# Fifteen instead of twelve weight pairs by seven products in the down projection, with GpSimd taking part of VectorE's work

## The chip, the cores and the metric

The kernel runs on one core of one Trainium2 chip. A core has TensorE (PE in the profile, with PEld for its weight loads), VectorE (DVE), ScalarE (ACT), GpSimd (POOL) and SyncE (SP), which here only issues DMAs. The metric is the device time of the core in microseconds, median of three runs; lower is better.

## The reference

One layer of an encoder block over 256 tokens of width 2048, in float32: RMS norm, one input projection, a bidirectional state-space mixer beside a pooling mixer, an output projection, a gated conv-MLP, and a gate by a per-layer embedding. The part that the change is about is the MLP and the gate after it:

```
hn = rmsnorm(h, ffn_norm_pre)
up = hn @ w_up                      # 256 x 2048 by 2048 x 11264
gate, val = split(up, 2)
hidden = gelu(dwconv3(gate)) * val  # 256 x 5632
h = h + rmsnorm(hidden @ w_down, ffn_norm_post)        # 5632 x 2048
gate = sigmoid(rmsnorm(h, ple_norm_pre) @ w_ple_gate)  # 2048 x 2048
out = h + rmsnorm(gate * (p @ w_ple), ple_norm_post)
```

## The kernel before, in words

**Products.** All large products keep float32 accuracy with a faster matmul type. Each operand is cut in a high part (the value rounded to float32r, a cast on ScalarE) and a low part (the value minus its high part, a subtraction on VectorE), and a product is the sum of three matmuls: high by high, high by low, low by high. `split` (lines 141 to 154) does this for a weight block; its two tags `whi` and `wlo` have five buffers each. Raw weights arrive in the tag `raw`, three buffers, by DMAs that SyncE issues in program order.

**Stages.** The input projection (dtu, xbc, z), the output projection (wo), the up projection (22 blocks of gate and 22 of value features, names ga and va, by `feature_pairs`), the down projection (dn), the small product ple, and the gate (gt). Down, gate and wo go by `token_major`: the 2048 output columns are done in two halves of 1024; in each half the loop goes over pairs of 128-row weight blocks. Down has 44 blocks, so 22 pairs per half, numbered u = 0 to 21. A half holds its sums in eight PSUM banks.

**Two ways for a pair.** A regular pair takes 2 blocks x 2 token halves x 2 column halves x 3 matmuls = 24 matmuls of 128x128 by 128x512, and two weight splits of 128x1024. A fast pair (listed in `dn_fast`, `gt_fast`) takes the 2x2 block product by seven products instead of eight (`seven_products`, from line 239), so 21 matmuls; it needs four weight splits (one of 128x512, three of 128x1024), of which two are of sums of weight blocks, and four sums of activation blocks with their own high and low parts (`pair_sums`, line 774: four small VectorE operations, a ScalarE cast, a VectorE subtraction). After the last fast pair of a half, `combine` (line 269) puts the products together once.

**Sums of weights.** `block_sums` (line 208) makes them ahead of time: during the up stage each of its jobs loads a 1 MB pair into a page, adds with three VectorE operations (`add_blocks`, lines 235 to 237), and stores the page to DRAM; down loads it back. The list `work` holds jobs by slot; `aside` runs one slot after each half of a `feature_pairs` call, 88 slots in up. There are 28 such pairs (24 of down, 4 of the gate), one every three slots; the last two stay in their pages.

**Activations of down.** `get_hid` (line 899) makes the high and low part of the 128x512 piece of the hidden activations that a pair needs, into the tag `hs` with two buffers: a cast on ScalarE (line 903) and a subtraction on VectorE (line 904). `hid_sums` makes the activation sums of a fast pair; in half 0 those of four pairs (`dn_keep`) are kept in pages and used again in half 1. Pages (tag `pg`, 13 buffers of 128x2048) hold the hidden activations (six), what is kept, and the loaded sums.

**Order.** A scheduler of the framework orders each engine's instructions in advance from estimated durations and priorities; each engine then runs its list strictly in order, with semaphores between engines.

**GpSimd before.** It does one multiplication per up slab (line 885), a few operations of the mixer (lines 673 and 685), the small norm factors, and in half 1 of down one DMA that adds in flight (`first_gate`, line 949). In down it is otherwise idle.

Of the kernel before, what the change touches and what calls it, by code (L numbers as in the profile page):

```python
# [16 lines left out]
P = 128  # L17
L = 256
# [33 lines left out]
def build(nc, a, out):  # L52
    x = a["x"][0]
    w_in, w_out, w_up = a["w_in"][0], a["w_out"][0], a["w_ffn_up"][0]
    w_down, w_gate, w_ple = a["w_ffn_down"][0], a["w_ple_gate"][0], a["w_ple"][0]
    out = out[0]

    with tile.TileContext(nc) as tc, \
# [37 lines left out]
        c_dt = DSSD + 1536  # L96
        r0 = wp.tile([P, 2048], F32, tag="raw", bufs=3, name="dtur0")
        for n in range(2):
            first = ins(nc.scalar.dma_start(r0[:, n * 352:(n + 1) * 352],
                                            w_in[:P, c_dt + n * 352:c_dt + (n + 1) * 352]))  # L100
# [55 lines left out]
        def raw(name, src, a_, b_):  # L156
            r = wp.tile([P, 2048], F32, tag="raw", bufs=3, name=name)
            if src is None:
                return r
            last["dma"] = load(r[:, :a_ * b_].rearrange("p (a b) -> p a b", a=a_), src, True)  # L160
            return r
# [46 lines left out]
        def block_sums(name, w, c0, k, held):  # L208


            pg = []

            def fetch():
                r = page(f"{name}b{c0}_{k}")
                pg.append(r)
                load(r.rearrange("p (k c) -> p k c", k=2),
                     w[k * P:(k + 2) * P, c0:c0 + 1024].rearrange("(k p) c -> p k c", p=P))
# [12 lines left out]
            return [fetch], [], [add], [store]  # L230
# [8 lines left out]
        def seven_products(name, stage, w, k0, c0, a_, acc, alt, start, stop):  # L239

            if (stage, c0, k0) in sums_:
                r = raw(f"{name}r", None, 0, 0)
                last["dma"] = load(r[:, 512:1536], w[(k0 + 1) * P:(k0 + 2) * P, c0:c0 + 1024], True)
                last["dma"] = load(r[:, :512], w[k0 * P:(k0 + 1) * P, c0:c0 + 512], True)
# [12 lines left out]
            t13 = split(f"{name}c", t[:, :1024], 1024)  # L259
            t42 = split(f"{name}d", t[:, 1024:], 1024)  # L260
            for x, (wh, wl), c, o, own in (
                    ("a11", b11, 0, alt[0], True), ("a12", b2, 0, acc[0][0], False), ("s4", b2, 512, acc[0][1], False),
                    ("s1", t13, 0, alt[1], True), ("s3", t13, 512, alt[2], True), ("a22", t42, 0, acc[1][0], False),
                    ("s2", t42, 512, alt[3], True)):
# [26 lines left out]
        def token_major(name, w, c0, ks, get, acc, tail=1, fast=(), alt=None, sums=None, at=()):  # L291
# [3 lines left out]
            for u in range(nu):  # L295
# [3 lines left out]
                if u in fast:  # L299
                    if u == fast[0]:  # L300
# [3 lines left out]
                r = None if f"{name}{k0}_0" in ready else raw(f"{name}r{k0}", w[k0 * P:(k0 + 2) * P, c0:c0 + 1024]  # L304
                                                               .rearrange("(k p) c -> p k c", p=P), 2, 1024)
# [17 lines left out]
        def feature_major(name, w, c0, get, acc):  # L323

            for u in range(4):
                r = raw(f"{name}r{u}", w[u * 512:(u + 1) * 512, c0:c0 + 512]
                        .rearrange("(k p) c -> p k c", p=P), 4, 512)
# [12 lines left out]
        def feature_pairs(name, w, c0, get, acc):  # L340


            for u in range(2):
                r = raw(f"{name}r{u}", w[u * 1024:(u + 1) * 1024, c0:c0 + 256]
                        .rearrange("(k p) c -> p k c", p=P), 8, 256)
# [97 lines left out]
        for u in range(0, NK, 2):  # L443
            r = [wp.tile([P, 2048], F32, tag="raw", bufs=3, name=f"dtur{u}") if u else r0, page(f"dtur{u + 1}")]
            for j in range(2):
                k = u + j
                if k == 0:
                    last["dma"] = load(r[0][:, 704:1056], w_in[:P, c_dt + 704:c_dt + 1056])
                    xload(1, 2)
                    x_panel(1, 2)  # L450
                    continue
                for c0, c1 in ((0, 704), (704, 1056)) if k == 1 else ((0, 1056),):
                    last["dma"] = load(r[j][:, c0:c1], w_in[k * P:(k + 1) * P, c_dt + c0:c_dt + c1])
# [29 lines left out]
        with tc.issue_after(half[0]), tc.issue_after(half[1]):  # L483
# [11 lines left out]
            for a_ in range(4):  # L495
# [17 lines left out]
        load(pmat.rearrange("p (g s t) -> p g s t", g=4, s=2),  # L513
             a["pool_matrix"].rearrange("g (s p) t -> p g s t", p=P))
        poolw = page("poolw")
        load(poolw.rearrange("p (g c d) -> p g c d", g=4, c=2),
             a["pool_w"][0].rearrange("g (c p) d -> p g c d", p=P))
# [122 lines left out]
        def xbc(slab):  # L640
            acc = main(f"xbc{slab}")
            feature_major(f"xb{slab}", w_in, DSSD + slab * 512, hn, acc)
# [88 lines left out]
        token_major("z", w_in, 0, list(range(NK)), hn, zacc)  # L731
# [42 lines left out]
        def pair_sums(name, s, o, a11, a21, a12, a22):  # L774

            s1, s2, s3, s4 = (s[:, i * P:(i + 1) * P] for i in range(4))
            nc.vector.tensor_sub(s1, a22, a21)
# [4 lines left out]
            nc.vector.tensor_sub(o[:, 512:], s[:, :512], o[:, :512].bitcast(F32))  # L782
            return {f"s{i + 1}": (o[:, i * P:(i + 1) * P], o[:, 512 + i * P:512 + (i + 1) * P]) for i in range(4)}
# [81 lines left out]
        dn_fast, gt_fast, dn_keep = ((2, 3, 5, 7, 8, 10, 12, 13, 15, 16, 18, 19), (2, 3, 5, 7, 8, 10, 12, 13, 15, 16, 18, 19)), ((4, 6), (1, 2)), (3, 8, 13, 18)  # L865
        gt_ks = list(range(NK)), [0, 1, 12, 13, 8, 9, 2, 3, 4, 5, 6, 7, 10, 11, 14, 15]
# [6 lines left out]
        hid = []  # L873
        for s in range(DFF // 512):
            sc = mid(f"gr{s}")
            for i in range(2):
                ga = main(f"ga{s}{i}")
                feature_pairs(f"ug{s}{i}", w_up, s * 512 + i * 256, hf, ga)
# [8 lines left out]
            for i in range(2):  # L887
                va = main(f"va{s}{i}")
                feature_pairs(f"uv{s}{i}", w_up, DFF + s * 512 + i * 256, hf, va)
# [9 lines left out]
        def get_hid(k):  # L899
            if k % 2 == 0:  # L900
                t = lp.tile([P, 1024], F32R, tag="hs", bufs=2, name=f"hs{k}")
                src = hid[k // 8][:, (k % 8) * L:(k % 8 + 2) * L]
                nc.scalar.copy(t[:, :512], src)  # L903
                nc.vector.tensor_sub(t[:, 512:], src, t[:, :512].bitcast(F32))  # L904
# [13 lines left out]
        keep, kept = [], {}  # L918

        def hid_sums(k):  # L920


            (h1, l1), (h2, l2) = get_hid(k), get_hid(k + 1)
            if k not in kept:
                src = hid[k // 8][:, (k % 8) * L:(k % 8 + 2) * L]
                n = dn_keep.index(k // 2) if k // 2 in dn_keep else -1
                if n >= 0 and n % 2 == 0:
                    keep.append(page(f"hsum{k}", F32R))
                o = keep[-1][:, n % 2 * 1024:(n % 2 + 1) * 1024] if n >= 0 else mid(f"he{k}", F32R)
                d = pair_sums(f"hd{k}", mid(f"hd{k}"), o, *(src[:, i * P:(i + 1) * P] for i in range(4)))  # L930
                if n >= 0:
                    kept[k] = d
            else:
                d = kept[k]
# [7 lines left out]

        def first_gate():

            r, hi, lo = page("gtf"), page("gtfh", F32R), page("gtfl", F32R)
            src = w_gate[:2 * P, :1024].rearrange("(k p) c -> p k c", p=P)
            last["dma"] = load(r.rearrange("p (k c) -> p k c", k=2), src)
            nc.scalar.activation(lo, r, AF.Copy, scale=-1.0)
            nc.gpsimd.dma_start(lo.rearrange("p (k c) -> p k c", k=2), src, accum_op=ALU.add)
            nc.scalar.copy(hi, r)  # L950
            for j in range(2):
# [3 lines left out]
                      fast=dn_fast, sums=hid_sums, at={13: back, 16: first_gate})  # L955
# [8 lines left out]
        vg = [page(f"vg{t}") for t in range(2)]  # L964
# [27 lines left out]
        for half in range(2):  # L992
# [12 lines left out]
            for t in range(2):  # L1005
                for n, (o, c0) in enumerate(columns(acc[t])):
# [15 lines left out]
                    else:  # L1022
                        nc.scalar.activation(so, sv, AF.Square, accum_out=q)
                    nc.vector.tensor_mul(vg[t][:, c], v, gple[:, c])
# [5 lines left out]
def laid_out(a):  # L1030

    def cols(*vs):
        return np.concatenate([v.reshape(-1, P).T for v in vs], axis=1)

    return {
        "x_cols": np.concatenate([cols(a["mix_norm_pre"][0]),
# [24 lines left out]
def constants():  # L1061
    return {"pool_matrix": pool_matrix()}
# [16 lines left out]
```

## Time and profile before

| | |
|---|---|
| median of 3 runs | 1123.48 us (1123.23 to 1123.48) |
| the profiled execution | 1123.11 us, of which the span is 1121.3 us |
| PE busy | 1109.1 us, 99% of the span |
| DVE, ACT, POOL busy | 925.2, 663.9, 76.2 us |
| mean granted TensorE clock | 0.997 |
| moved by DMA | 300.87 MB, mean 268 GB/s |

The profile is of one execution. Busy PE means that matmuls were in its pipeline; a matmul's own duration overlaps that of the next, so the rate is read from the length of an uninterrupted stretch and its count, not from the mean of one. Durations of VectorE operations overlap a little too: what one costs the engine is the distance from its start to the start of the next, where they run without a gap. The up stage runs from about 309 to 789 us, down from 789 to 1016.7 us (its halves divide at about 902.6 us), ple and gate to the end.

### The profile page before, as it was taken

The page shows a single profiled execution, that of the slowest core. Times are in us where ns is not written, and L with a number is a line of the kernel's source. Part 1 is how long each engine was busy: PE and PEld are TensorE (multiplying, and loading weights), DVE is VectorE, ACT ScalarE, POOL GpSimd, SP SyncE. Part 2 cuts the span into 40 slices and gives each one's busy share as a digit, 9 for nine tenths or more (in the row PEclk, how much of TensorE's full clock was granted, in tenths as well). Part 3 has the DMA queues.
Part 4 walks back from the last instruction along what each step waited for, and adds up shares of the span by engine and source line. Part 5 has one row for each costly group of instructions (what it writes and reads, how often), then busy time and mean ns, then how long its engine had stood idle before and what let it go on. Part 6 is the DMA issues. An engine that isn't in the chain of part 4 may idle for free.

```text
span 1121.3 us, 15775 instructions
## 1 busy us (share of the span) xinstructions
PE 1109.1 (99%) x5971; PEld 956.4 (85%) x5971; DVE 925.2 (83%) x1275; ACT 663.9 (59%) x927; POOL 76.2 (7%) x86
## 2 busy tenths in 40 slices
PE   9999999999999999999999999999999999999996
PEld 9999987888888888888888888888888888888875
DVE  6569895799898877877877768888899999889795
ACT  6847663555764554554545445445677777786672
POOL 0200004200110100000000000000000000001001
PEclk9999999999999999999999999999999999999998
DMA  9862447456789989989999898996969688995663
GB/s 363 310 207 96 170 161 269 151 188 190 252 308 347 328 300 336 314 289 309 333 330 314 276 330 289 325 304 224 339 185 334 221 286 301 383 318 177 230 235 109
DMA packets 145996, 300.87 MB, mean 268 GB/s; under 512 B 5504, under 2 KB 98560, under 8 KB 137856
## 3 DMA queue, kind: packets, MB, share of 16 engines
q1 hardware_dynamic: 145360, 298.45, 78.6%
q0 software_dynamic: 272, 1.05, 0.5%
q8 instruction: 47, 0.77, 0.3%
q10 hardware_dynamic: 288, 0.36, 0.1%
q14 instruction: 29, 0.24, 0.1%
HBM read 268.38 MB, written 31.46 MB: 267 GB/s over the span
## 4 chain that ended last, share of the span: by engine, by line
PE 96%; ACT 1%; DVE 1%; issue 1%; POOL 1%; POOLq 0%; DVEq 0%; ACTq 0%
PE va L87 22%; PE ga L87 21%; PE dna L87 14%; PE woa L87 7%; PE xbc L87 6%; PE gt L87 5%; PE dtu L87 4%; PE z L87 4%; PE dns L87 3%; PE dn0s L87 1%; PE dn1s L87 1%; PE ple L87 1%; PE pw L87 1%; PE yd L87 0%; PE gts L87 0%
## 5 line engine op out<-in xcount | busy, mean ns | idle before, releaser
L87 PE MATMUL ga<-wox,ug_0h 128*128 128x512 f32 x352 | 125.5, 395 | 0.0
L87 PE MATMUL ga<-wox,ug_1h 128*128 128x512 f32 x352 | 125.1, 394 | 0.0
L87 PE MATMUL va<-wox,uv_1h 128*128 128x512 f32 x352 | 124.8, 393 | 0.0
L87 PE MATMUL va<-wox,uv_0h 128*128 128x512 f32 x352 | 124.8, 393 | 0.0
L87 PE MATMUL ga<-wox,ug_1l 128*128 128x256 f32 x352 | 99.1, 282 | 0.0
L87 PE MATMUL ga<-wox,ug_0l 128*128 128x256 f32 x352 | 99.1, 282 | 0.0
L87 PE MATMUL va<-wox,uv_1l 128*128 128x256 f32 x352 | 99.1, 281 | 0.0
L87 PE MATMUL va<-wox,uv_0l 128*128 128x256 f32 x352 | 99.1, 281 | 0.0
L87 PEld LDWEIGHTS va<-wox,uv_1h 128*128 128x128 f32 x352 | 66.1, 188 | 15.0
L87 PEld LDWEIGHTS va<-wox,uv_0h 128*128 128x128 f32 x352 | 66.1, 188 | 15.0
L87 PEld LDWEIGHTS ga<-wox,ug_0h 128*128 128x128 f32 x352 | 66.1, 188 | 14.9
L87 PEld LDWEIGHTS ga<-wox,ug_1h 128*128 128x128 f32 x352 | 66.1, 188 | 14.9
L87 PEld LDWEIGHTS ga<-wox,ug_0l 128*128 128x128 f32 x352 | 66.2, 188 | 0.1
L87 PEld LDWEIGHTS ga<-wox,ug_1l 128*128 128x128 f32 x352 | 66.2, 188 | 0.0
L87 PEld LDWEIGHTS va<-wox,uv_0l 128*128 128x128 f32 x352 | 66.2, 188 | 0.0
L87 PEld LDWEIGHTS va<-wox,uv_1l 128*128 128x128 f32 x352 | 66.2, 188 | 0.0
L885 POOL TENSOR_TENSOR fc<-fc,rfb 128x1024 f32<-128x1024 f32 x11 | 28.0, 2547 | 438.6 <-ACT fc L884 438.6
L87 PE MATMUL dna<-dn_0h,hs 128*128 128x512 f32 x160 | 50.1, 393 | 0.0
L87 PE MATMUL dna<-dn_1h,hs 128*128 128x512 f32 x160 | 49.9, 393 | 0.0
L235 DVE TENSOR_TENSOR dnb<-dnb 128x1024 f32<-128x1024 f32 x24 | 30.8, 1283 | 17.8 <-DMA dnb<-w_ffn_down 17.6
L903 ACT CAST hs<-hid 128x512 fp32r<-128x512 f32 x44 | 27.2, 617 | 23.2 <-PE dna L87 14.8
L904 DVE TENSOR_TENSOR hs<-hid,hs 128x512 fp32r<-128x512 f32 x44 | 30.2, 686 | 9.8 <-ACT hs L903 9.7
(1903 smaller groups left out, 3105.3 us busy)
## 6 DMA issues: line engine op xcount, KB each, us to landing
dnb<-w_ffn_down SPq DMA_DIRECT2D x24, 1024.0 KB, 10.4
dns<-dnb SPq DMA_DIRECT2D x22, 1024.0 KB, 7.4
dn0r<-w_ffn_down SPq DMA_DIRECT2D x10, 1024.0 KB, 6.0
dn1r<-w_ffn_down SPq DMA_DIRECT2D x10, 1024.0 KB, 7.1
zr<-w_in SPq DMA_DIRECT2D x8, 1024.0 KB, 5.1
dtur<-w_in SPq DMA_DIRECT2D x14, 528.0 KB, 8.7
wo0r<-w_out SPq DMA_DIRECT2D x7, 1024.0 KB, 5.6
wo1r<-w_out SPq DMA_DIRECT2D x6, 1024.0 KB, 5.5
```

What stands on the lines that cost most here:

```text
L87: last["pe"] = ins(nc.tensor.matmul(o, lhsT, rhs, start=start, stop=stop, skip_group_check=True))
L235: nc.vector.tensor_add(v[:, 0:2], v[:, 0:2], v[:, 1::2])
L885: nc.gpsimd.tensor_tensor(cv.rearrange("p (f t) -> p f t", f=4), cv.rearrange("p (f t) -> p f t", f=4), rfb.unsqueeze(1).to_broadcast([P, ...
L903: nc.scalar.copy(t[:, :512], src)
L904: nc.vector.tensor_sub(t[:, 512:], src, t[:, :512].bitcast(F32))
```

## The change

Seven edits come together.

1. Fast pairs of down: 15 of 22 per half instead of 12; the gate's first half has three fast pairs instead of two (five in all). The list of weight pairs whose sums are made in up grows from 28 to 35, one every 12/5 slots instead of every three.
2. The low part of the hidden activations (`get_hid`) is subtracted on GpSimd instead of VectorE, in all 22 pairs of both halves.
3. The activation sums of the four kept pairs (4, 9, 14, 18) are made by jobs during up and stored to DRAM (512 KB each); half 0 of down loads them into two pages, and half 1 uses these again.
4. The host lays every weight out in tiles, so that a 1 MB load is contiguous: 8 KB per partition, where it was runs of 1 KB (up), 2 KB (xbc) or 4 KB (down, gate, wo, z).
5. The seven products go in another order (a11, a12, a22, s4, s2, s1, s3), with the split of the sums `d` ahead of `c`.
6. The first gate weights are loaded at pair 16 of half 1 as before, their split is moved to pair 18.
7. The pages of the gate's result are taken when first written.

```diff
             else:
-                r = t = raw(f"{name}r", w[k0 * P:(k0 + 2) * P, c0:c0 + 1024]
-                            .rearrange("(k p) c -> p k c", p=P), 2, 1024)
+                r = t = raw(f"{name}r", w[c0 // 1024, k0 // 2])
...
+            t42 = split(f"{name}d", t[:, 1024:], 1024)
             t13 = split(f"{name}c", t[:, :1024], 1024)
-            t42 = split(f"{name}d", t[:, 1024:], 1024)
...
-        dn_fast, gt_fast, dn_keep = ((2, 3, 5, 7, 8, 10, 12, 13, 15, 16, 18, 19), (2, 3, 5, 7, 8, 10, 12, 13, 15, 16, 18, 19)), ((4, 6), (1, 2)), (3, 8, 13, 18)
-        gt_ks = list(range(NK)), [0, 1, 12, 13, 8, 9, 2, 3, 4, 5, 6, 7, 10, 11, 14, 15]
+        dn_fast, gt_fast = ((2, 3, 4, 5, 6, 8, 9, 10, 11, 13, 14, 15, 16, 18, 19), (2, 3, 4, 5, 6, 8, 9, 10, 11, 13, 14, 15, 16, 18, 19)), ((4, 5, 6), (1, 2))
+
+        dn_keep = (4, 9, 14, 18)
+        gt_ks = list(range(NK)), [0, 1, 8, 9, 10, 11, 2, 3, 4, 5, 6, 7, 12, 13, 14, 15]
...
-                work[3 * i + 2 + j].extend(jobs)
+                work[12 * i // 5 + 2 + j].extend(jobs)
...
+        def hid_sums_jobs(k):
+
+            o = []
+
+            def make():
+                o.append(lp.tile([P, 1024], F32R, tag="hs", bufs=2, name=f"he{k}"))
+                pair_sums(f"he{k}", o[0][:, 512:].bitcast(F32), o[0],
+                          *(hid_part(k)[:, i * P:(i + 1) * P] for i in range(4)))
+
+            def store():
+                kept[k] = dp.tile([P, 1024], F32, tag=f"hsum{k}", bufs=1, name=f"hsum{k}")
+                load(kept[k], o[0].bitcast(F32))
+
+            return [make], [store]
...
-                nc.scalar.copy(t[:, :512], src)
-                nc.vector.tensor_sub(t[:, 512:], src, t[:, :512].bitcast(F32))
+                nc.scalar.copy(t[:, :512], hid_part(k))
+                nc.gpsimd.tensor_sub(t[:, 512:], hid_part(k), t[:, :512].bitcast(F32))
...
-                      fast=dn_fast, sums=hid_sums, at={13: back, 16: first_gate})
+                      fast=dn_fast, sums=hid_sums, at={13: back, 16: first_load, 18: first_gate})
```

More of the change, by code (lines that the diff above doesn't have):

```diff
@@ L916, in hid_get @@
             return hcache[k]
-        keep, kept = [], {}
         def hid_sums(k):
             (h1, l1), (h2, l2) = get_hid(k), get_hid(k + 1)
[L924 to L927, printed above, removed]
-                    keep.append(page(f"hsum{k}", F32R))
[L929 to L934, printed above, removed]
+            d = kept.get(k)
+            if d is None:
+                d = pair_sums(f"hd{k}", mid(f"hd{k}"), mid(f"he{k}", F32R),
+                              *(hid_part(k)[:, i * P:(i + 1) * P] for i in range(4)))
+            elif not isinstance(d, dict):
+                n = dn_keep.index(k // 2)
+                if n % 2 == 0:
+                    keep.append(page(f"hsum{k}", F32R))
+                o = keep[-1][:, n % 2 * 1024:(n % 2 + 1) * 1024]
+                last["dma"] = load(o.bitcast(F32), d, True)
+                d = kept[k] = sums_in(o)
             return dict(d, a11=(h1[:, :P], l1[:, :P]), a12=(h2[:, :P], l2[:, :P]), a22=(h2[:, P:], l2[:, P:]))
@@ L963, in build @@
         gple = gload("gple", a["ple_norm_post"][0])
-        vg = [page(f"vg{t}") for t in range(2)]
+        vg = []
         sq = [[], []]
```

103 lines of the change are left out of this document (59 added, 44 removed).

## The prediction

> **What bounds the kernel now.** I read the page first: busy shares, then the chain of waits. TensorE is busy for 99% of the span and the chain lies on it for 96%, so I looked for its rate in the stage that changes. The chain of waits (start us, length us, engine, tile, line, count):
>
> ```profile
> PE 1109.1 (99%) x5971; PEld 956.4 (85%) x5971; DVE 925.2 (83%) x1275; ACT 663.9 (59%) x927; POOL 76.2 (7%) x86
> 788.96 11.11 PE dna L87 x48
> ...
> 891.49 22.16 PE dna L87 x96
> ...
> 1016.74 3.45 PE ple L87 x15
> ```
>
> 96 matmuls of 512 columns in 22.16 us are 0.231 us each. Down has 20 regular pairs of 24 and 24 fast pairs of 21, together 984 matmuls, 227.1 us at that rate; from 788.96 to 1016.74 it took 227.8. So down runs at TensorE's rate with 0.7 us lost, and fewer matmuls can shorten it, if what feeds TensorE keeps pace. The busy times of the engines by stage tell how near it is (stretch, us, PE, PEld, DVE, ACT, POOL busy with counts, PE clock, DMA share, GB/s); the last two rows are the two halves of down:
>
> ```profile
> 309.00:420.00 111.00, 111.00 (x638) 97.35 (x638) 94.01 (x120) 60.39 (x81) 9.19 (x5) 1.00 0.96 322
> 420.00:530.00 110.00, 110.00 (x632) 96.56 (x632) 86.14 (x107) 53.54 (x70) 4.81 (x2) 1.00 0.93 311
> 530.00:640.00 110.00, 110.00 (x632) 96.56 (x631) 85.42 (x108) 53.14 (x72) 4.80 (x2) 1.00 0.97 317
> 640.00:789.00 149.00, 149.00 (x855) 130.78 (x854) 121.41 (x159) 75.44 (x102) 9.95 (x4) 1.00 0.89 290
> 935.00:965.00 30.00, 30.00 (x131) 24.36 (x130) 27.24 (x39) 19.89 (x26) 0.00 (x0) 1.00 0.93 351
> 1016.70:1050.00 33.30, 33.30 (x162) 27.11 (x161) 28.86 (x49) 23.40 (x39) 4.61 (x10) 1.00 0.67 224
> 1050.00:1085.00 35.00, 34.57 (x150) 27.83 (x149) 30.70 (x37) 25.10 (x35) 1.30 (x2) 1.00 0.70 236
> 789.00:902.60 113.60, 113.60 (x493) 92.32 (x492) 105.33 (x147) 81.75 (x108) 0.00 (x0) 1.00 0.77 261
> 902.60:1016.70 114.10, 114.05 (x494) 92.29 (x493) 104.67 (x143) 84.46 (x109) 3.78 (x8) 1.00 0.91 323
> ```
>
> VectorE is busy for 210.0 of 227.7 us in down, 92%: it is the second bound, and the question of the change is what VectorE has to do afterwards. ScalarE has 27% to spare there, and in up TensorE never waits.
>
> **The change part by part.** The matmuls removed: six pairs of down go from 24 to 21, 18 x 0.231 = 4.15 us; one pair of the gate, 0.69 us. Down then has 966 matmuls, 223.0 us. If nothing else moved, the profiled execution's 1123.1 us (0.37 below the median of the runs shown) would become 1118.3.
>
> VectorE in down, from the distance of starts where its operations follow without a gap (start us, us, engine, line, operation):
>
> ```profile
> 812.72 0.28 DVE L777 TENSOR_TENSOR hd<-hid 128x128 f32<-128x128 f32 x1
> ...
> 813.65 1.22 DVE L153 TENSOR_TENSOR dn010dl<-dn010t,dn010dh 128x1024 fp32r<-128x1024 f32 x1
> ...
> 818.74 0.68 DVE L904 TENSOR_TENSOR hs<-hid,hs 128x512 fp32r<-128x512 f32 x1
> 819.34 0.68 DVE L153 TENSOR_TENSOR dn014al<-dn014r,dn014ah 128x512 fp32r<-128x512 f32 x1
> 819.95 1.22 DVE L153 TENSOR_TENSOR dn014bl<-dn014r,dn014bh 128x1024 fp32r<-128x1024 f32 x1
> 821.08 0.68 DVE L904 TENSOR_TENSOR hs<-hid,hs 128x512 fp32r<-128x512 f32 x1
> ```
>
> A low part of 512 costs 0.60 us, one of 1024 1.13, the four small operations of an activation sum 0.93, its low part 0.60. Removed: 44 low parts of the hidden activations, 44 x 0.60 = 26.4. Added: a pair that turns fast has one low part of 512 and three of 1024 in place of two, 0.60 + 1.13 = 1.73, six times, 10.4. Activation sums made in down: 12 + 8 before, 11 + 11 after, two more at 1.53, 3.1. VectorE's own work in down becomes 210.0 - 26.4 + 10.4 + 3.1 = 197.1 us, 88% of 223.0. By this count alone the change fits.
>
> But the 44 subtractions now run on GpSimd, beside a VectorE that is nearly always busy. Up has eleven GpSimd operations beside VectorE ones. Two of these places in the order of time, then the durations (min/median/max ns) of the eleven and of the four of the size that the change adds:
>
> ```profile
> 372.36 0.69 DVE L236 TENSOR_TENSOR dnb<-dnb 128x512 f32<-128x512 f32 x1
> 372.43 2.89 POOL L885 TENSOR_TENSOR fc<-fc,rfb 128x1024 f32<-128x1024 f32 x1 [40.30 <-ACT fc L884]
> 373.09 2.78 DVE L237 TENSOR_TENSOR dnb<-dnb 128x512 f32<-128x512 f32 x1
> 375.79 1.21 DVE L153 TENSOR_TENSOR uv_0l<-uv11r,uv_0h 128x1024 fp32r<-128x1024 f32 x1
> ...
> 462.08 2.41 POOL L885 TENSOR_TENSOR fc<-fc,rfb 128x1024 f32<-128x1024 f32 x1 [42.56 <-ACT fc L884]
> 463.33 2.24 DVE L153 TENSOR_TENSOR uv_1l<-uv31r,uv_1h 128x1024 fp32r<-128x1024 f32 x1 [1.41 <-ACT uv_1h L152]
> ...
> L885 POOL TENSOR_TENSOR fc<-fc,rfb x11: 2394/2407/3168, 329.0 to 774.6; 128x1024 f32<-128x1024 f32 x11
> L685 POOL TENSOR_TENSOR y<-y,ym x4: 1262/1821/2180, 178.3 to 199.8; 128x512 f32<-128x512 f32 x4
> ```
>
> The addition at 373.09 takes 2.78 us in place of 0.69 and ends 0.55 after GpSimd does (375.32); the low part at 463.33 takes 2.24 in place of 1.22 and ends 1.08 after it (464.49). So a VectorE operation that comes up while GpSimd works stands still until GpSimd is done. It also shows who goes first when both wait: GpSimd's operation came 0.07 us after VectorE's first addition, was held for the rest of it (2.89 in place of 2.40) and ran ahead of the second. In the first place the operation after the addition would have started at 372.36 + 2 x 0.60 = 373.56 and started at 375.79: 2.23 us lost to an operation of 2.40, 0.93 of it. In the second 1.02 us were lost of the 1.16 that GpSimd still had, 0.88. One of 128x512 takes 1.26 us undisturbed, so it costs a busy VectorE 1.11 to 1.17, at most the whole 1.26; a gain is excluded, as neither place shows an operation shortened. I take 1.15, nearer the first place, where VectorE had work waiting throughout as it has in down. 44 x 1.15 = 50.6 us come in for the 26.4 that went, and VectorE is occupied or held for 247.7 us against TensorE's 223.0. A fast pair with sums needs 0.60 + 3 x 1.13 + 1.53 + 1.15 = 6.67 us of it, TensorE 4.85; five such run in a row, and five weight buffers hold little more than one pair. VectorE becomes the bound of down.
>
> The Trainium skill, SBUF — State Buffer, section Who interferes with whom, says that a VectorE instruction with two SBUF inputs and a GpSimd instruction that reads SBUF exclude each other for the whole instruction. By its rule the price would be all of 1.26, 55.5 in sum, and the time 1144 instead of 1139; the rows agree with the exclusion and fall short of the whole instruction by a tenth.
>
> Part of the excess is taken from VectorE's lead. It begins on pair 2 at 789.57, and TensorE ends pairs 0 and 1 only at 788.96 + 11.11 = 800.07:
>
> ```profile
> 789.57 0.69 DVE L153 TENSOR_TENSOR dn04al<-dn04r,dn04ah 128x512 fp32r<-128x512 f32 x1
> ```
>
> That is 10.5 us, of which at least the 6 matmuls behind the last split, 1.4, must remain: a credit of at most 9.1, and of nothing if the buffers, full at that moment, make VectorE idle meanwhile. I take 4, near the middle, as either extreme would have it always or never blocked there. Down becomes 247.7 - 4 = 243.7 us, 15.9 more than now. Ends: 1.11 with 9.1 gives 236.8 (+9.0), 1.26 with nothing 252.6 (+24.8).
>
> Gate: the fifth pair has 1.73 more of splits and one more set of activation sums (an addition of 512 ahead of it, 0.60 + 1.53), 3.9 us of VectorE, which has 4.4 and 4.3 us idle in the two gate rows; TensorE already lost 0.43 there. Between -0.7 (all hidden) and +3.2; I take 0, as about 0.7 will show.
>
> Up: seven more weight sums and four activation sums.
>
> ```profile
> L235 DVE TENSOR_TENSOR dnb<-dnb 128x1024 f32<-128x1024 f32 x24 | 30.8, 1283 | 17.8 <-DMA dnb<-w_ffn_down 17.6
> L237 DVE TENSOR_TENSOR dnb<-dnb 128x512 f32<-128x512 f32 x24 | 18.6, 774 | 0.3
> L236 DVE TENSOR_TENSOR dnb<-dnb 128x512 f32<-128x512 f32 x24 | 16.4, 685 | 0.2
> L903 ACT CAST hs<-hid 128x512 fp32r<-128x512 f32 x44 | 27.2, 617 | 23.2 <-PE dna L87 14.8
> ```
>
> 7 x 2.74 + 4 x 1.53 = 25.3 us more, on 387 of 480: 86%. The additions stand in VectorE's order and hold the splits behind them while their load is late (17.6 us over eleven waits now), without TensorE waiting once. I take 0; the upper end is the rival on transfers. Tiles by the host, the products' order and the later pages change no count of TensorE, which waits for no DMA now: 0. The queues: on GpSimd the low parts stand behind the in-flight DMA of the first gate weights and the norm factors, and behind ScalarE's cast (0.62 us). With a11, a12, a22 first, an `hs` buffer is free after 9 of 21 matmuls, so the next piece has 12 x 0.231 + 4.85 = 7.6 us for cast, at most one VectorE operation and the 1.26: covered, and GpSimd is not late itself. ScalarE's part of an activation sum and of a split grows like VectorE's and has the 27%.
>
> Sum: 1123.1 + 15.9 + 0 + 0 = 1139 us.
>
> **Rivals.** (1) GpSimd costs VectorE little, and the time falls to 1118.3. TensorE stays the bound if 197.1 + 44 x price is at most 223.0 + 4, a price of 0.68; equal time comes at 0.79. For it: the busy counts alone. Against it: both quoted places show 0.88 or more of GpSimd's time lost. A price in between gives 1119 to 1132.
>
> (2) The transfers of up become its bound. Its four rows move 308 GB/s at a share of 0.93, 330 if full. Seven sums are loaded and stored, 14.7 MB, and four activation sums stored, 2.1: 34 GB/s over some 490 us, 342 in all. At 330 up grows by 3.7%, 18 us, and the sum is 1157. Against it: the stretch from 935 us, with longer runs, moves 351 at 0.93, 377 if full, and tiles make all runs long; up is then full to 0.91. The Trainium skill, DMA: Bandwidth & Descriptors, section Specifications, gives line rate from 512 B per run on; by that the tiles would raise nothing and the 1157 would come. The two rates here speak against it.
>
> (3) The tiles bring time by themselves. TensorE waits for no DMA in any row, so nothing but the start could gain; I give it no chance of its own.
>
> **How the numbers follow.** The forecast, VectorE held by GpSimd, 0.76, by itself 1132 to 1150; rival 1 0.11; a price in between 0.05; rival 2 0.08. A change of 0.2%, 2.2 us, is about the least a measurement of this kernel can tell. Slower: 0.76 + 0.08 + 0.02 of the price in between, 0.86; faster 0.12; within 0.02. The range from 1125 to 1152 holds the forecast's own and the greater part of the prices in between; rival 1 and most of rival 2 lie outside.
>
> **What would show it.** Right: 44 GpSimd subtractions in down of 1.3 to 2.4 us; VectorE low parts of 1024 beside them near 2.3 us instead of 1.22; TensorE waiting for VectorE low parts in the fast runs, some 20 us together; VectorE busy for over 97% of down. The gate at its present length, up without a wait of TensorE, its DMA share near 0.9. Wrong: low parts that stay at 1.22 beside GpSimd, and down at 223 us; or up longer than 480 us for the same matmuls, with DMA at 0.97 or more.

## The result, and the profile after

The changed kernel takes 1174.62 us, median of 6 runs (1170.24 to 1176.44), against 1123.36 (1123.13 to 1123.58) for the kernel before on the same chip: 1.0452 times as long, 95% interval 1.0432 to 1.0471. It is slower, as forecast, but by 51 us and not by 16.

The profiled execution took 1176.44 us, its span 1174.6, 53.3 more than before. The busy times and the shares of the chain of waits, from the page of the changed kernel:

```profile
PE 1130.1 (96%) x5950; PEld 954.5 (81%) x5950; DVE 975.9 (83%) x1302; ACT 675.1 (57%) x948; POOL 155.1 (13%) x130
...
PE 71%; DVE 14%; issue 5%; ACT 5%; DMA 3%; POOL 1%; SPq 0%; DVEq 0%; POOLq 0%; ACTq 0%
```

TensorE had 21 matmuls fewer and was busy 21.0 us longer (1130.1 against 1109.1), and 29% of the chain now lies on others, where it was 4%. To find the stage, I took the start of down's first and last matmul in each trace. Before: 788.8 and 1016.3; after: 818.6 and 1069.6. So up ends 29.8 us later, down takes 251.0 in place of 227.5, 23.5 more, and what follows takes 105.0 in both. 29.8 + 23.5 + 0 = 53.3. The busy times by engine for these stretches (stretch, us, PE, PEld, DVE, ACT, POOL busy with counts, PE clock, DMA share, GB/s), first up and down before, then after:

```profile
309.00:788.80 479.80, 479.80 (x2752) 421.07 (x2752) 386.99 (x492) 242.31 (x322) 28.75 (x13) 1.00 0.93 308
788.80:1016.70 227.90, 227.85 (x988) 184.79 (x987) 210.00 (x288) 166.40 (x216) 3.78 (x8) 1.00 0.84 292
```

```profile
309.00:818.60 509.60, 493.86 (x2754) 426.38 (x2754) 407.63 (x526) 237.53 (x325) 40.86 (x15) 0.98 0.84 323
818.70:1070.00 251.30, 235.55 (x970) 177.86 (x969) 236.72 (x273) 179.86 (x231) 69.09 (x48) 1.00 0.80 291
```

In up the same matmuls keep TensorE busy 14.1 us longer and leave it idle for 15.7. VectorE has spare time there (80%) and the DMA share fell. In down VectorE went up to 94%, not over 97%. What TensorE waited for in up, from the chain of waits (start us, length us, what; the first part of an unbroken run of calls), and in sum (us in total, times, longest):

```profile
423.22 12.56 PE va L88 x62
435.77 10.85 PE ga L88 x62
...
446.70 0.38 ACT gr L353
...
447.11 0.76 DVE gr L354 x2
...
447.89 0.70 DVE gr L902
...
449.72 0.94 ACT ug_0h L151
...
452.56 1.21 DVE ug_0l L152
```

```profile
PE ga L88 <- DVE ug_0l L152: 5.2, 8, 0.8
PE ga L88 <- ACT ug_0h L151: 4.8, 4, 1.9
PE va L88 <- ACT uv_0h L151: 3.5, 4, 1.1
PE va L88 <- DVE uv_0l L152: 2.1, 4, 0.5
```

Before, TensorE waited for nothing in up. Now the chain goes from TensorE's last matmul of a call to ScalarE's copy that empties its sums (L353), VectorE's addition (L354), and from there to the split of the next weights. VectorE at that place, by the timeline (start us, us, engine, line, operation, in brackets idle time and what ended it), after and before:

```profile
447.11 0.75 DVE L354 TENSOR_TENSOR gr<-gr,ga 128x256 f32<-128x256 f32 x2 [3.56 <-ACT gr L353]
447.89 0.69 DVE L902 TENSOR_TENSOR gr<-gr,rfb 128x512 f32<-128x512 f32 x1
448.50 1.22 DVE L232 TENSOR_TENSOR dnb<-dnb 128x1024 f32<-128x1024 f32 x1
449.64 1.66 DVE L422 SCALAR_TENSOR_TENSOR fc<-gr,vt,fc 128x255 f32<-128x255 f32 x4
451.21 0.68 DVE L233 TENSOR_TENSOR dnb<-dnb 128x512 f32<-128x512 f32 x1
451.93 0.69 DVE L234 TENSOR_TENSOR dnb<-dnb 128x512 f32<-128x512 f32 x1
452.54 1.22 DVE L152 TENSOR_TENSOR ug_0l<-ug31r,ug_0h 128x1024 fp32r<-128x1024 f32 x1
```

```profile
440.95 1.23 DVE L153 TENSOR_TENSOR ug_1l<-ug31r,ug_1h 128x1024 fp32r<-128x1024 f32 x1 [1.52 <-ACT ug_1h L152]
442.92 0.42 DVE L360 TENSOR_TENSOR gr<-gr,ga 128x256 f32<-128x256 f32 x1 [0.74 <-ACT gr L359]
443.87 1.23 DVE L153 TENSOR_TENSOR uv_0l<-uv30r,uv_0h 128x1024 fp32r<-128x1024 f32 x1 [0.53 <-ACT uv_0h L152]
```

After, VectorE idles 3.56 us for the copy that waits for TensorE, then adds the copied sums, does the norm, the convolution and three additions of weights (5.43 us from 447.11 to 452.54), and only then the next low part (`ug_0l`, of the call that TensorE is already in). Before, that call's last low part, `ug_1l`, was made ahead of the emptying. I counted in VectorE's order how many of the four splits of the next call stand ahead of each emptying of the sums; each feeds 16 matmuls. A call has 64; the 2752 of the 479.8 us are 43 calls of 11.2 us, so a split is worth 2.8 us of TensorE. Before: 4 almost throughout, mean 3.9 over the 44 emptyings (the last has no next call and counts as 0). After: 2, 2, 2, 2, 1, 0 again and again, mean 1.8. This is the first theory for up, below "the order"; its rival is the prediction's own, transfers or VectorE's work. For down, the theory is that of the prediction: GpSimd holds VectorE.

### The profile page after: what moved, and what is told of

It is laid out like the page before. It is cut to its first block, busy times and chain, and to the rows that moved or that the text cites. A ratio compares the mean times of both kernels' runs of the same rounds, so it can differ in the third digit from the quotient of the medians.

```text
span 1174.6 us, 15891 instructions
## 1 busy us (share of the span) xinstructions
PE 1130.1 (96%) x5950; PEld 954.5 (81%) x5950; DVE 975.9 (83%) x1302; ACT 675.1 (57%) x948; POOL 155.1 (13%) x130
## 4 chain that ended last, share of the span: by engine, by line
PE 71%; DVE 14%; issue 5%; ACT 5%; DMA 3%; POOL 1%; SPq 0%; DVEq 0%; POOLq 0%; ACTq 0%
PE va L88 18%; PE ga L88 15%; PE woa L88 7%; PE dna L88 6%; PE xbc L88 5%; PE gt L88 4%; PE dtu L88 4%; PE z L88 4%; PE dns L88 1%; DMA ug81r<-w_up 1%; DVE he L775 1%; DMA dnb<-w_down 1%; DVE ug_0l L152 1%; PE dn0s L88 1%; DMA ug51r<-w_up 1%
## 5 line engine op out<-in xcount | busy, mean ns | idle before, releaser
L88 PE MATMUL ga<-wox,ug_0h 128*128 128x512 f32 x352 | 129.3, 407 | 4.8 <-ACT ug_0h L151 4.8
L923 POOL TENSOR_TENSOR hs<-hid,hs 128x512 fp32r<-128x512 f32 x44 | 71.2, 1619 | 192.1 <-ACT hs L922 192.1
L905 POOL TENSOR_TENSOR fc<-fc,rfb 128x1024 f32<-128x1024 f32 x11 | 33.3, 3031 | 448.4 <-ACT fc L904 448.4
L88 PEld LDWEIGHTS va<-wox,uv_0h 128*128 128x128 f32 x352 | 66.1, 190 | 19.1 <-ACT uv_0h L151 4.8
L353 ACT COPY gr<-ga 128x256 f32<-128x256 f32 x44 | 15.6, 377 | 107.3 <-PE ga L88 107.3
L353 ACT COPY hid<-va 128x256 f32<-128x256 f32 x44 | 16.0, 373 | 85.8 <-PE va L88 85.7
L354 DVE TENSOR_TENSOR gr<-gr,ga 128x256 f32<-128x256 f32 x44 | 17.1, 419 | 48.3 <-ACT gr L353 48.3
```

Source lines behind the costliest of these rows:

```text
L88: last["pe"] = ins(nc.tensor.matmul(o, lhsT, rhs, start=start, stop=stop, skip_group_check=True))
L353: nc.scalar.copy(o[:, f * L:(f + 1) * L], acc[f][:, L:])
L354: nc.vector.tensor_add(o[:, f * L:(f + 1) * L], o[:, f * L:(f + 1) * L], acc[f][:, :L])
L905: nc.gpsimd.tensor_tensor(cv.rearrange("p (f t) -> p f t", f=4), cv.rearrange("p (f t) -> p f t", f=4), rfb.unsqueeze(1).to_broadcast([P, ...
L923: nc.gpsimd.tensor_sub(t[:, 512:], hid_part(k), t[:, :512].bitcast(F32))
```

## The experiments

A table of the stages of all kernels stands at the end of this section.

**e1, the order put back, all work kept.** What follows a call (emptying, norm, convolution) is issued in the next call, behind its last split. Each call's four splits then stand ahead of it. The activation sums made in up move by two slots, as what they read is ready later.

```diff
+                    if u == 1 and j == 1 and pending:
+                        with tc.issue_after(last["act"]), tc.issue_after(last["dve"]):
+                            pending.pop(0)()
...
-                work[u // 2 * 8 + u % 2 * 2 + 6 + j].extend(jobs)
+                work[u // 2 * 8 + u % 2 * 2 + 8 + j].extend(jobs)
...
-                total(o, ga)
...
+                pending.append(job(gate_part, s, i, sc, ga))
```

> The changed kernel with one thing added: in up, the operations that take a finished accumulation out of PSUM (and what follows on them) are placed in the lists of ScalarE and VectorE behind all four weight splits of the next feature_pairs call, as they stood before the change; work, bytes and sums stay as in the changed kernel. Theory A (up grew by 30 us because the recorded order has the next call's splits behind operations that wait for TensorE): up returns from 525 to about 496 us, down stays near 251, total about 1145 us. Theory B (up is limited by the transfers of seven more sums): up stays near 525, total about 1174. Theory C (VectorE has too much to do in up): the same as B.

Measured: 1147.41 us, 1.0213 [1.0196, 1.0230] of before. The windows of up and down, as above:

```profile
309.00:789.00 480.00, 480.00 (x2753) 421.34 (x2753) 411.55 (x527) 242.81 (x325) 40.74 (x15) 1.00 0.88 344
789.00:1040.80 251.80, 236.52 (x971) 179.18 (x970) 236.39 (x273) 180.06 (x231) 68.58 (x48) 0.99 0.81 289
```

Up is back at TensorE's rate, with VectorE's work of the changed kernel (411.55 us, 24.6 more than before) and at 344 GB/s, the rate that the second rival needed (342). So neither work nor transfers made up longer. VectorE at the same place:

```profile
446.55 1.23 DVE L152 TENSOR_TENSOR ug_0l<-ug31r,ug_0h 128x1024 fp32r<-128x1024 f32 x1 [0.97 <-ACT ug_0h L151]
447.69 1.22 DVE L152 TENSOR_TENSOR ug_1l<-ug31r,ug_1h 128x1024 fp32r<-128x1024 f32 x1
448.83 0.75 DVE L357 TENSOR_TENSOR gr<-gr,ga 128x256 f32<-128x256 f32 x2
```

Both splits of the call now come ahead of the emptying (L357), and VectorE does not idle 3.56 us for it. Down stays as in the changed kernel.

**e2, the low parts back on VectorE, order as changed.**

```diff
-                nc.gpsimd.tensor_sub(t[:, 512:], hid_part(k), t[:, :512].bitcast(F32))
+                nc.vector.tensor_sub(t[:, 512:], hid_part(k), t[:, :512].bitcast(F32))
```

> The changed kernel with the low parts of the hidden activations back on VectorE; nothing else. Theory A (GpSimd's 44 subtractions hold VectorE for over 1.1 us each, and VectorE bounds down): up stays at 525 us, down falls from 251 to 225 to 230, as VectorE then has 197.1 + 26.4 = 223.5 us of work against TensorE's 223.0; total about 1150 us. Rival (the three more fast pairs load VectorE and GpSimd is only beside it): down grows or stays at 250 or more, total 1174 or above.

Measured: 1155.57 us, 1.0282 [1.0257, 1.0307]. Up still ends 26.9 us late, so GpSimd's part in down does not cause that; down fell from 251.0 to 231.8, a little above the 225 to 230 expected.

**e4, both undone.** e1 and e2 together, that is 15 fast pairs with 35 sums in up and the low parts on VectorE.

> The changed kernel with both: the order of e1 in up and the low parts on VectorE. If the order and GpSimd are the two causes and there is no third, up is about 496 us, down 225 to 230, the gate as before: total 1119 to 1126, at or a little under the kernel before. If something else of the change costs time, it stays above 1130.

Measured: 1128.19 us, 1.0042 [1.0027, 1.0057], above the 1119 to 1126 expected of two causes alone. Up is at 480, and down:

```profile
789.00:1021.80 232.80, 229.36 (x971) 181.34 (x970) 220.98 (x315) 178.04 (x231) 3.82 (x6) 0.99 0.86 313
```

Against e1 this differs in GpSimd alone: 1145.5 - 1126.4 = 19.1 us of span. The low parts of 1024 of the regular pairs in half 0 and half 1, by tile (count: min/median/max ns), first e1, then e4:

```profile
L152 DVE TENSOR_TENSOR dn_1l<-dn0r,dn_1h x7: 1206/2314/2322, 781.8 to 904.3; 128x1024 fp32r<-128x1024 f32 x7
L152 DVE TENSOR_TENSOR dn_1l<-dn1r,dn_1h x7: 1209/1716/2320, 909.8 to 1036.2; 128x1024 fp32r<-128x1024 f32 x7
```

```profile
L152 DVE TENSOR_TENSOR dn_1l<-dn0r,dn_1h x7: 1215/1217/1226, 781.9 to 895.6; 128x1024 fp32r<-128x1024 f32 x7
L152 DVE TENSOR_TENSOR dn_1l<-dn1r,dn_1h x7: 1212/1218/1221, 899.1 to 1017.2; 128x1024 fp32r<-128x1024 f32 x7
```

The same instruction takes 1.22 us, or up to 2.32 beside a subtraction of GpSimd. Two of the 44 low parts run ahead of down in the kernels compared here, so e4's 315 operations of VectorE are e1's 273 and 42 low parts. VectorE's own work in e1's down is then e4's less 42 x 0.60: 220.98 - 25.2 = 195.8. It was busy for 236.39, so 40.6 us are held time, 0.97 per subtraction. Even with both causes undone 15 pairs are 4.8 us slower than 12 in down (232.3 against 227.5).

**e3, GpSimd alone in the kernel before.**

```diff
-                nc.vector.tensor_sub(t[:, 512:], src, t[:, :512].bitcast(F32))
+                nc.gpsimd.tensor_sub(t[:, 512:], src, t[:, :512].bitcast(F32))
```

> The kernel before with only the low parts of the hidden activations moved to GpSimd. VectorE's own work in down falls from 210.0 to 183.6 us. By the price of the prediction, 1.15 us a subtraction, it is occupied for 234.2 us and down takes about 230: total 1126. By a price of 1.3, which would explain the changed kernel's 251 us of down, 240.8 us: total 1131 to 1136. If GpSimd costs VectorE nothing: no change, 1123.

Measured: 1129.03 us, 1.0050 [1.0035, 1.0065]; down 231.5, 4.0 more, with VectorE busy as follows:

```profile
788.60:1020.40 231.80, 229.79 (x987) 183.62 (x986) 221.69 (x245) 165.50 (x216) 74.07 (x49) 1.00 0.83 287
```

VectorE had 25.2 us less to do (184.8) and was busy for 11.7 more: (221.69 - 184.8) / 42 = 0.88 per subtraction. That is less than the prediction's 1.15, and down is still 1.5 us longer than the 230 expected by 1.15, as VectorE idled for 10.1 us. The move alone makes the kernel before slower.

**e5, the subtraction on both engines**, in the kernel before: GpSimd does it a second time into a tile that nothing reads, so no one waits for its result.

```diff
+                dup = sp.tile([P, 512], F32, tag="junk", bufs=1, name=f"dup{k}")
+                nc.gpsimd.tensor_sub(dup, src, t[:, :512].bitcast(F32))
```

> The kernel before, and beside each of VectorE's 44 low parts of the hidden activations GpSimd does the same subtraction once more into a tile that nobody reads; VectorE keeps all its work. So only GpSimd's price is added. By 0.9 us a subtraction (what e1 against e4 and e3 against before leave) VectorE is held for 40 us more, 250 in down, and with 12 to 15 us of gaps down is 262 to 265 us: total 1157 to 1161. By the prediction's 1.15: 50.6 more, total 1168 to 1172. If only the low parts that wait for GpSimd matter and not the port: 1123.

Measured: 1153.18 us, 1.0264 [1.0243, 1.0284]; down 257.1:

```profile
789.00:1046.50 257.50, 238.29 (x988) 184.38 (x987) 251.86 (x288) 166.16 (x216) 78.78 (x50) 0.99 0.77 259
```

(251.86 - 210.00) / 42 = 1.00 per subtraction, the same work otherwise. The cost needs no wait for GpSimd's result; running beside VectorE is enough. The total is below the 1157 to 1161 expected by 0.9, as VectorE idled for only 5.6 us and not for 12 to 15.

**e11, GpSimd writing only**: three settings to zero in place of e5's subtraction.

```diff
-                nc.gpsimd.tensor_sub(dup, src, t[:, :512].bitcast(F32))
+                for _ in range(3):
+                    nc.gpsimd.memset(dup, 0.0)
```

> As e5, but GpSimd writes zeros to the tile three times instead of subtracting, so it works beside VectorE in down without reading SBUF. If what holds VectorE is the reading, as the Trainium skill, SBUF — State Buffer, section Who interferes with whom, has it: 1123 to 1125. If any GpSimd operation on SBUF holds VectorE: 15 us or more longer.

Measured: 1128.53 us, 1.0043 [1.0028, 1.0058], but down is 227.5 as before. Its second half:

```profile
902.60:1021.00 118.40, 118.35 (x513) 95.89 (x512) 109.35 (x148) 87.83 (x116) 37.12 (x71) 1.00 0.88 314
```

66 of the 132 settings run there, one behind the other from 909.08 to 947.66 us; the other 66 ran ahead of down. GpSimd is busy for 37.12 us, against 3.78 before, and VectorE is not held: 210.04 us for the 288 operations of down, 210.00 before. A row of GpSimd's timeline (start us, us) shows where the 5.5 us of span went:

```profile
289.74 20.98 POOL L907 MEMSET dup<- 128x512 f32 x36
```

36 settings ran ahead of the norm factors of the up stage, whose first matmul on values came at 325.2 in place of 319.7. The Trainium skill, SBUF — State Buffer, section Who interferes with whom, says that a VectorE instruction with two SBUF inputs contends with a GpSimd instruction that reads SBUF and not with one that only writes it. e5 and e11 agree, 29.6 us in down against none, though e11's settings cover only some 39 us of it.

**e6, up's weights without tiles**, e1 with runs of 1 KB as before.

```diff
-                r = raw(f"{name}r{u}", w[u])
+                r = raw(f"{name}r{u}")
+                last["dma"] = load(r.rearrange("p (a b) -> p a b", a=8), w[0][u * 1024:(u + 1) * 1024, w[1]:w[1] + 256]
+                                   .rearrange("(k p) c -> p k c", p=P), True)
```

> e1 (the changed kernel, order of up put right) with w_up left as it came, runs of 1 KB, the other weights in tiles. Theory B, the prediction's second rival: at 330 GB/s for such runs up needs 342 and grows by some 18 us over e1, total about 1165, with a DMA share near 1.0 in up. Theory A, transfers have room either way: as e1, 1147.

Measured: 1147.17 us, 1.0210 [1.0195, 1.0225], the time of e1. Up:

```profile
309.00:789.00 480.00, 480.00 (x2753) 421.29 (x2752) 410.73 (x526) 242.07 (x326) 40.73 (x15) 1.00 0.98 344
```

344 GB/s also with short runs, at a share of 0.98 in place of e1's 0.88: the second rival falls with tiles (e1) and without (e6). The tiles make transfers shorter, not the kernel.

**e7, tiles and order of products alone**, the changed kernel with the 12 pairs, the 28 sums, the four gate pairs and the low parts of before.

```diff
-                work[12 * i // 5 + 2 + j].extend(jobs)
+                work[3 * i + 2 + j].extend(jobs)
...
-                nc.gpsimd.tensor_sub(t[:, 512:], hid_part(k), t[:, :512].bitcast(F32))
+                nc.vector.tensor_sub(t[:, 512:], hid_part(k), t[:, :512].bitcast(F32))
```

> The changed kernel with the lists of before (12 pairs a half, 28 sums every three slots, four gate pairs), the kept activation sums made in half 0 and the low parts on VectorE: what is left of the change is the tiles, the order of the seven products and the later pages. By the prediction these bring nothing: 1123, with a DMA share some tenth lower in up. If tiles bring time by themselves: under 1121.

Measured: 1124.00 us, 1.0004 [0.9994, 1.0014]: no time in them. The DMA share in up falls to 0.83, and 3.9 splits stand ahead of an emptying, as before.

**e9, the order alone, no work added**: e7, with the splits put behind the emptying where the changed kernel has them, so that the numbers ahead are the same call by call.

```diff
+        lead = [4, 3, 4, 4, 2, 2, 2, 2, 2, 1, 0, 2, 2, 2, 2, 1, 0, 2, 2, 2, 2, 1, 0, 2, 2, 2, 2, 1, 0, 2, 2, 2, 2, 1, 0, 2, 2, 2, 2, 2, 0, 2, 4, 0]
...
-                    wh, wl = split(f"{name}{u}_{j}", r[:, j * 1024:(j + 1) * 1024], 1024)
+                    with ExitStack() as behind:
+                        if fin and 2 * u + j >= lead[fin["t"]]:
+                            behind.enter_context(tc.issue_after(fin["act"]))
+                            behind.enter_context(tc.issue_after(fin["dve"]))
+                        wh, wl = split(f"{name}{u}_{j}", r[:, j * 1024:(j + 1) * 1024], 1024)
```

> e7 (work, sums and bytes of the kernel before, 1124 us) with one thing imposed: in up the weight splits of each feature_pairs call are put behind the emptying of the accumulation before, as far as they stand behind it in the changed kernel (4, 3, 4, 4, then mostly 2, and 1 and 0 twice in every 24 splits or so, instead of 4 throughout). Theory A (the order alone costs up its 30 us): up grows by 15 to 30 us with no operation or byte added, total 1139 to 1154. Theory B or C (transfers or VectorE's work): up stays at 496, total 1124.

Measured: 1145.47 us, 1.0205 [1.0190, 1.0221]. Up:

```profile
309.00:809.00 500.00, 486.88 (x2752) 423.21 (x2752) 376.31 (x493) 233.62 (x322) 38.64 (x13) 0.99 0.80 296
```

With 28 sums and 296 GB/s up ends 20.3 us later than before: the order by itself does it. It gives two thirds of the 29.8. Of the 9.5 left, 5.1 go with TensorE's granted clock (last section): e9's up has two stretches of 3.4 us at half clock, 3.4 us lost, the changed kernel's loses 8.5. Where else the changed kernel's order differs (the additions between emptying and split, the loads) was not separated.

**e10, 32 sums**: e2 with 14 pairs a half, four gate pairs and one job pair every 81/31 slots.

```diff
-                work[12 * i // 5 + 2 + j].extend(jobs)
+                work[81 * i // 31 + 2 + j].extend(jobs)
```

> e2 with 14 fast pairs a half and four in the gate, so 32 sums made in up instead of 35, spaced evenly; the recorded order then has 2.3 splits ahead of an emptying on average (the kernel before 3.9, the changed kernel 1.8). Theory A: up grows over 496 us, but less than the 27 us of e2: by 8 to 20. Down, VectorE lighter by about 6 us than in e2: 226 to 230. Total 1132 to 1146.

Measured: 1136.32 us, 1.0115 [1.0096, 1.0133]. The mean number of splits ahead is 2.3, between 3.9 and 1.8, and up ends 10.3 us late, between 0 and 26.9 (e2):

```profile
309.00:799.00 490.00, 483.97 (x2753) 422.05 (x2752) 403.59 (x519) 237.64 (x325) 37.85 (x13) 1.00 0.85 326
```

**e8 and e12, in search of a version that gains.** e8 is e4 with the activation sums of five more pairs made in up, stored, and loaded in both halves, so that VectorE has 11 us less to do in down.

```diff
-        dn_keep = (4, 9, 14, 18)
+        dn_keep, dn_more = (4, 9, 14, 18), (3, 6, 10, 13, 16)
...
+            elif k // 2 in dn_more:
+                o = mid(f"he{k}", F32R)
+                last["dma"] = load(o.bitcast(F32), d, True)
+                d = sums_in(o)
```

> e4 (order put right, low parts on VectorE, 15 pairs) with the activation sums of five more pairs (3, 6, 10, 13, 16) made in up and loaded in both halves of down. If VectorE alone keeps e4 at 232 us of down, its 221 us of work fall by 2 x 5 x 1.53 = 15.3 to 206, with some 12 of gaps 218, under TensorE's 223: down 224 to 227, total 1119 to 1122, below the kernel before. If the transfers bound down (5.2 MB more, share now 0.85 to 0.88), it stays at 1128 or above.

Measured: 1134.29 us, 1.0094 [1.0079, 1.0109]: slower than e4, by a down of 238.9 with VectorE busy for 209.96 of it. In its chain of waits and its sum of TensorE's waits stand:

```profile
923.76 7.64 DMA dn112r<-w_down
```

```profile
PE dns L88 <- ACT dn132ah L151: 3.6, 1, 3.6
```

A load of weights that takes 7.64 us and a late cast are part of it. VectorE idled for 28.9 us, against 11.8 in e4; its longest waits in sum, e8 and then e4, are for the cast of the hidden activations:

```profile
DVE hs L936 <- ACT hs L935: 13.3, 14, 2.2
```

```profile
DVE hs L936 <- ACT hs L935: 4.2, 6, 1.8
```

What makes these casts late was not tried, so the rest stays open. e12 is e4 with 13 pairs a half, (2, 3, 5, 7, 8, 10, 11, 12, 13, 15, 16, 18, 19), four gate pairs and 30 sums, one every 81/29 slots:

```diff
-                work[12 * i // 5 + 2 + j].extend(jobs)
+                work[81 * i // 29 + 2 + j].extend(jobs)
```

> e4 with 13 fast pairs a half, four in the gate and 30 sums: order of up put right, low parts on VectorE, four pairs' activation sums made in up. TensorE has 978 matmuls in down, 225.7 us, VectorE some 209 and 12 of gaps, 221. If both bounds hold, down takes 226 to 227 and the total is 1121.5 to 1123, at most a little under the kernel before; if VectorE's gaps grow with the sums it is 1124 or above.

Measured: 1123.45 us, 1.0003 [0.9995, 1.0012]; down 227.4, above the 226 to 227 expected, though TensorE has 6 matmuls, 1.4 us, less than before. None of the versions beats the kernel before.

The stages of all kernels, us: start of down's first matmul, down from its first to its last matmul's start, what follows, and the whole span.

| kernel | down starts | down | rest | span |
|---|---|---|---|---|
| before | 788.8 | 227.5 | 105.0 | 1121.3 |
| after | 818.6 | 251.0 | 105.0 | 1174.6 |
| e1 order back | 789.0 | 251.4 | 105.1 | 1145.5 |
| e2 low parts on VectorE | 815.7 | 231.8 | 105.1 | 1152.6 |
| e3 before, low parts on GpSimd | 788.6 | 231.5 | 106.3 | 1126.4 |
| e4 both undone | 789.1 | 232.3 | 105.0 | 1126.4 |
| e5 before, subtraction twice | 789.0 | 257.1 | 105.4 | 1151.5 |
| e6 order back, up untiled | 788.8 | 251.1 | 105.0 | 1144.9 |
| e7 tiles alone | 789.6 | 226.8 | 106.3 | 1122.7 |
| e8 more sums in up | 788.6 | 238.9 | 104.9 | 1132.4 |
| e9 order alone | 809.1 | 227.2 | 106.3 | 1142.6 |
| e10 32 sums | 799.1 | 230.3 | 105.4 | 1134.8 |
| e11 settings only | 794.3 | 227.5 | 105.0 | 1126.8 |
| e12 13 pairs | 788.9 | 227.4 | 105.4 | 1121.7 |

## Why the prediction was right and wrong

**The step that failed** is "Up: seven more weight sums and four activation sums ... I take 0; the upper end is the rival on transfers". It costs 29.8 us, more than half of the loss, by a mechanism that the prediction did not name. The prediction saw that the additions hold the splits behind them, and took from the trace of before that this costs TensorE nothing. It asked whether VectorE had the time (86% forecast, 411.55 of 480 in e1: it had) and whether the transfers had the rate (342 forecast, 344 in e1 and e6: they had). It did not ask where the new operations go in an order written in advance. The chain is: with the sums added, the recorded order puts the next call's splits behind the emptying of the sums; the emptying waits for TensorE's last matmul of the call; while VectorE and ScalarE do what follows, TensorE uses up the one or two splits it has, and stops. e1 takes 29.6 us away by the order alone, e9 brings 20.3 by the order alone. That the scheduler ordered it so because the added work raised its estimates was not tried by itself; the runs show only that 28 sums left 3.9 splits ahead, 32 sums 2.3 and 35 sums 1.8.

The trace of before had the rows to ask it (the low part at 440.95 ahead of the emptying at 442.92): TensorE's lead in up is what keeps it from waiting. The text of the prediction priced such a lead in down ("a credit of at most 9.1") but not in up.

**Down: right mechanism, sizes off.** Forecast +15.9, measured +23.5; in e1, where up is undisturbed, +23.9. Term by term in e1's down: VectorE's own work 195.8, forecast 197.1; held time 40.6, forecast 50.6, as a subtraction costs 0.97 (0.88 in e3, 1.00 in e5) and not 1.15, and 42 run in down and not 44; and idle time of VectorE 251.8 - 236.4 = 15.4, where the forecast had a lead that would take 4 off. So two terms were off in opposite directions, 10 us too much held time and 19.4 us too little idle time, and that 251.4 still lies inside the ends given for down, 236.8 to 252.6, is partly luck. The idle time is the worse of the two: 243.7 assumed that a VectorE that is the bound does not wait. It waits, longest for casts of ScalarE (us in total, times, longest; e1, down):

```profile
DVE dn132al L152 <- ACT dn132ah L151: 3.4, 1, 3.4
DVE dn06al L152 <- ACT dn06ah L151: 1.6, 1, 1.6
DVE dn132dl L152 <- ACT dn132dh L151: 1.5, 1, 1.5
```

In e4 it idles too, 232.8 - 221.0 = 11.8 us, and 15 pairs do not pay there even without GpSimd: the forecast's count of 223.0 for TensorE was not reached by any kernel with 15 pairs. Why is not shown; less work for VectorE did not help (e8). The prediction's "five such run in a row" was a misreading, on which no term of the sum rests: of pairs 2 to 6, pair 4 has its activation sums from up.

**Signs that were forecast.** The 44 subtractions, by tile:

```profile
L923 POOL TENSOR_TENSOR hs<-hid,hs x44: 1280/1331/5043, 762.8 to 1056.2; 128x512 fp32r<-128x512 f32 x44
```

1.3 to 2.4 us in down was forecast: right, the median is 1.33 and the longest in down 2.34 (the 5.04 is one of the two that ran ahead of down). Low parts of 1024 near 2.3: right in half 0 (median 2.31 in e1), not in half 1 (1.72). TensorE waiting for low parts some 20 us: it idled for 15.7 in down, of which 13.5 ended with an operation of VectorE. VectorE over 97% of down: wrong, 94%. Up without a wait of TensorE: wrong, 15.7 us idle. Its DMA share near 0.9: 0.84, and 0.88 in e1; up longer than 480 us, a sign of being wrong, came, but without the share of 0.97 named beside it. The gate at its length: right, 105.0 from down's end in both; tiles and order of products nothing: right, e7.

**Rivals.** The first, GpSimd free, falls by e1 against e4, 19.1 us. A price in between is nearer to what came, 0.88 to 1.00; its total of 1119 to 1132 did not come, as VectorE's idle time and up were added. The whole instruction, 1.26, which the prediction set against its 1.15, did not come either. The second, transfers, would have given a time nearer to the result (1157) for a reason that e1 and e6 exclude: the rate of 330 that it took as full was exceeded at 344. By the rule of the Trainium skill (DMA: Bandwidth & Descriptors, section Specifications: line rate from 512 B per run on) tiles raise nothing and 1157 would come. It did not come. Both runs moved 344 GB/s in the same 480 us, but with the DMA engines busy for 0.98 of the time without tiles and 0.88 with them; so for the time that they were busy tiles did raise the rate. The third, tiles bringing time, falls by e7.

## What to carry to other kernels

Where each engine runs a fixed list, check after any added work how many prepared operands stand ahead of every instruction that waits for the consumer; an engine at 80% can starve the one that it feeds. Try an operation moved from VectorE to GpSimd alone: here it took 0.88 to 1.00 us from VectorE and freed 0.60. When a bound moves to another engine, add that engine's own waits to its work: here they were 5.6 to 15.4 us of down.

## What the runs showed of the hardware

A short wait can cost TensorE more than its length. After the waits around 494 us its granted clock fell (windows as above; the changed kernel):

```profile
479.00:489.00 10.00, 10.00 (x60) 8.79 (x58) 6.71 (x9) 3.57 (x5) 0.00 (x0) 1.00 0.82 319
489.00:499.00 10.00, 8.36 (x37) 6.70 (x36) 6.25 (x8) 6.24 (x9) 0.00 (x0) 0.83 0.92 330
...
779.00:789.00 10.00, 7.43 (x25) 5.81 (x25) 10.00 (x16) 6.98 (x10) 0.00 (x0) 0.66 0.96 370
```

In the second row TensorE was idle for 1.64 us of the ten and ran 37 matmuls in place of 60, at a mean clock of 0.83; in windows of 1 us the clock is 1.00 up to 495, 0.50 from 496 to 498 and 1.00 again from 499. In the whole of up there are four such stretches, after waits near 423, 494, 637 and 782 us, of 3.4, 3.4, 3.4 and 6.8 us at half clock. They lose 8.5 us, which is most of the 14.1 that TensorE was busy longer. Waits as long as those near 423 us, 1.06 and 0.53 us close together, left the clock at 1.00 near 566 and 710 us, so their length alone does not decide it. The Trainium skill, TensorE: Matmul & The Clock Gate, section What's actually happening, says that the clock goes to half after an idle window of about 3.4 us, for at least one such window. The stretches of 3.4 us at half clock agree. A loss of 0.17 of 10 us is what half speed for 3.4 us would give, an estimate from that page; the idle time here was shorter than the window it names.

A GpSimd operation that only writes did not hold VectorE (e11); one that reads held it for about three quarters of its own shortest time (0.97 of 1.28 us in e1). With up's weights in runs of 1 KB all transfers of up together moved 344 GB/s over 480 us (e6), as with runs of 8 KB (e1), with the DMA engines busy for 0.98 of the time in place of 0.88.
